# Six Strassen pairs per MLP instead of four, squares on ScalarE, and eight low parts made by ScalarE and an adding DMA

## The chip, the cores and the metric

The kernel runs on one core of one Trainium2 chip. The metric is the device time of one execution, in microseconds; three runs of the kernel before took 555.92, 555.95 and 556.19 us. Beside them one execution was taken by the hardware profiler.

## The reference

A causal decoder trunk of two layers on 256 tokens of width 1024, in float32. Layer 0 mixes tokens with block-sparse attention of 16 heads (one block of 256 here), layer 1 with dilated attention of 12 heads in three groups. Each mixer is followed by a squared-ReLU MLP, and each of the four sub-layers is post-normalised:

```python
def sq_relu_mlp(x, w_in, w_out):                 # w_in 1024 x 4096, w_out 4096 x 1024
    return jnp.square(jax.nn.relu(x @ w_in)) @ w_out

for i in range(2):
    mix = moba_attention(h, ...) if i % 2 == 0 else dilated_attention(h, ...)
    h = layer_norm(2 ** 0.5 * h + mix, ...)
    h = layer_norm(2 ** 0.5 * h + sq_relu_mlp(h, w_in[i], w_out[i]), ...)
```

(2 ** 0.5 is DEEPNORM_ALPHA for a depth of 2.)

## The kernel before

**Split numbers.** Every large product is made of three products of a faster float type: an operand a is stored as a high part (rounded) and a low part (a minus its high part), and a*b is taken as hi*hi + hi*lo + lo*hi. `split` (line 378) does this: ScalarE (ACT) copies the source into the high tile (line 380), VectorE (DVE) subtracts (line 385). `load_w` (394) brings one weight tile of 128 x 1024 (512 KB) into a "raw" buffer with a DMA of the SP queue and splits it into a "whi" and a "wlo" tile. There are 7 raw buffers and 10 of each of the others.

**The MLP** (class `Mlp`, 1062) works on the 4096 hidden columns in eight chunks of 512. `head` does the x @ w_in part of chunk 0 in a token-major form while the LayerNorm ahead of the MLP is being finished. A step "f" followed by a chunk's number does it for one other chunk (`do_first`): four weight tiles of 128 hidden columns each, products into four "tp" banks of PSUM (`mm_wstat_wide`, 523: 8 of 512 columns and 8 of 256 for each tile), and behind each bank `relu_sq` (1040): an ACT copy of half the bank, a DVE addition, and a DVE operation that takes max(u, 0) * u. `relu_sq_T` splits the result into "ahi" and "alo".

A step "o" (`do_out`) is the second matmul of one chunk: four weight tiles of w_out, each with 24 / 2 = 12 products of 512 columns (two halves of tokens m, two halves of the output columns, three terms; `mm_rows`, 637) into the four "acc" banks. The tiles of the tail (`ntail`, the last 4 of MLP 0 and 6 of MLP 1) wait for `out_and_ln` (998), which does the four banks one after the other so that the LayerNorm of token half 0 (`ln_half`, 961) can start while half 1 is still on TensorE. In the last MLP half 1 has a form of its own: a right part of 256 columns, the left 512, and the last 256 on top of what DVE puts into a further bank; then `ln_last` (930).

**Strassen pairs.** Two weight tiles (256 hidden units) against two halves of tokens and two halves of columns are a 2 x 2 block product. A step "S" (`do_duo`, 1121) does it with seven block products of three terms (21 products of 512 columns) instead of eight (24). Before that, four sums of blocks of weights are made by DVE and split (`load_duo`, 597), and four sums of blocks of activations (`duo_sums`, 572). Four of the seven products collect in the four "tp" banks over all Strassen pairs of the MLP, so no "f" step can come after the first S; step "z" (`combine`, 1139) adds them to the residual rows, one ACT copy and eight DVE operations. Chunks 4 and 5 are done in this way:

```python
STEPS = ("f1 o0 f2 o1 f3 o2 f4 f5 f6 f7 S40 o3 S42 o6 S50 S52 z o7",) * 2   # written twice in the file
```

**What sets the order.** The program text makes a list of operations with their reads and writes. `Plan.order` (179) gives each a due time and plays them through a model of the engines; on each engine the ready one with the earliest due time goes first. TensorE's due times follow the program text, and the loads on SP stay in its order. The stores of the last LayerNorm's half 0 are given due times 8 and 7 us ahead of the end (`store`, 926, `early`). The resulting order is written out for each engine; waits are semaphores. At step f4 the kernel also loads the LayerNorm's g and b, and in MLP 0 the rope table and the mask of layer 1.

Behind MLP 0's last products TensorE goes on with `layer1_head` (1276): the first value projection of layer 1 for token half 0.

Of the kernel before, what the change touches and what calls it, by code (L numbers as in the profile page):

```python
# [319 lines left out]
def tile_trunk(  # L320
# [248 lines left out]
    def split_part(n, src, sk, hi, lo, hk, lk, sbuf=True):  # L569
        split(n, src, hi, lo, sk, hk, lk, sbuf=sbuf)  # L570

    def duo_sums(hk, hk2):

        a11, a21 = part(hk, S, P), part(hk, S + P, P)
        a12, a22 = part(hk2, S, P), part(hk2, S + P, P)
# [1 line left out]
        s1, s2, s3, s4 = [part(s, i * P, P) for i in range(4)]
        rk, rk2 = [(hk, 1)], [(hk2, 1)]
        tt(P, s3, a11, a21, ALU.subtract, rk, [(s, 2)])
        tt(P, s1, a21, a22, ALU.add, rk + rk2, [(s, 0)])  # L580
        tt(P, s2, a22, s3, ALU.subtract, rk2 + [(s, 2)], [(s, 1)])
        tt(P, s4, a12, s2, ALU.subtract, rk2 + [(s, 1)], [(s, 3)])
        tags = [duo_tags[(len(duo_used) * 4 + i) % len(duo_tags)] for i in range(4)]
        duo_used.append(s)
        (ph, pl), (sh, sl) = [[mk([P, 512], F32R, *tags[2 * i + h]) for h in range(2)] for i in range(2)]
        split(P, a11, part(ph, 0, P), part(pl, 0, P), rk, [(ph, 0)], [(pl, 0)], sbuf=True)
        split(S, part(hk2, S, S), part(ph, P, S), part(pl, P, S), rk2, [(ph, 1)], [(pl, 1)], sbuf=True)
        split(512, lambda: s.t, lambda: sh.t, lambda: sl.t, [(s, i) for i in range(4)], [(sh, 0)], [(sl, 0)], sbuf=True)
        one = [(ph, pl, i * P, int(i > 0)) for i in range(3)]
        four = [(sh, sl, i * P, 0) for i in range(4)]  # L590
        return one + four

    duo_tags = [("sc0", 4), ("sc0", 4), ("sc0", 4), ("sc0", 4), ("sc1", 4), ("sc1", 4), ("sc1", 4), ("sc1", 4),
                ("v", 4), ("v", 4), ("v", 4), ("v", 4), ("q0hi", 1), ("q0lo", 1), ("q1hi", 1), ("q1lo", 1)]
    duo_used = []

    def load_duo(x_src, y_src, single):

        x = mk([P, 1024], F32, "raw", NRAW)
        dma(lambda: x.t, x_src, (), [(x, 0)], P * 1024 * 4)  # L600
        b11, b12 = part(x, 0, 512), part(x, 512, 512)
# [1 line left out]
        split(512, b11, part(hi, q * 512, 512), part(lo, q * 512, 512), [(x, 0)], [(hi, q)], [(lo, q)], sbuf=True)
        y = load_w(y_src)
        b22, b21 = part(y.raw, 0, 512), part(y.raw, 512, 512)
        yk = [(y.raw, 0)]
        ts = [mk([P, 512], F32, tag, 2) for tag in ("pt0", "pt1", "pt0", "pt1")]
        t1, t3, t2, t4 = ts
        pairs = [[mk([P, 1024], F32R, tag, NSLOT) for tag in ("whi", "wlo")] for _ in range(2)]

        def put(t, i):
            h, l = pairs[i // 2]
            c = i % 2
            split(512, lambda: t.t, part(h, c * 512, 512), part(l, c * 512, 512), [t], [(h, c)], [(l, c)], sbuf=True)
            return h, l, c * 512, c

        whole = lambda t: (lambda: t.t)
        tt(512, whole(t1), b12, b11, ALU.subtract, [(x, 0)], [t1])
        tt(512, whole(t3), b22, b12, ALU.subtract, yk + [(x, 0)], [t3])
        w5, w7 = put(t1, 0), put(t3, 1)  # L620
        tt(512, whole(t2), b22, whole(t1), ALU.subtract, yk + [t1], [t2])
        w6 = put(t2, 2)
        tt(512, whole(t4), b21, whole(t2), ALU.subtract, yk + [t2], [t4])
        w4 = put(t4, 3)
        return (hi, lo, q * 512, q), (y.hi, y.lo, 512, 0), (y.hi, y.lo, 0, 0), w4, w5, w6, w7
# [406 lines left out]
    def relu_sq_T(ps, ahi, alo, j):  # L1032
        both, hk = relu_sq(ps)
        keys = [(j, 0), (j, 1)]
        split(
            S, part(both, S, S), lambda: ahi.t[:, j, :], lambda: alo.t[:, j, :], hk,
            [(ahi, k) for k in keys], [(alo, k) for k in keys], sbuf=True,
        )

    def relu_sq(ps):  # L1040
        both = mk([P, 512], F32, "ta", NTA)
        u, h = (lambda: both.t[:, :S]), (lambda: both.t[:, S:])
        uk, hk = [(both, 0)], [(both, 1)]
        op("ACT", act(S), lambda: nc.scalar.activation(u(), ps.t[:, S:], AF.Copy), [ps], uk)  # L1044
        tt(S, u, lambda: ps.t[:, :S], u, ALU.add, [ps] + uk, uk)
        stt(S, 0, h, u, lambda: 0.0, u, ALU.max, ALU.mult, uk, hk)
        return both, hk
# [14 lines left out]
    class Mlp:  # L1062
# [17 lines left out]
        def rest(self, between):  # L1080
# [8 lines left out]
            def do_out(c):
                for j in range(4):  # L1090
                    pos = c * 4 + j
                    item = ((*chunks[c], j), load_w(wout[i][pos]), pos, nkt)
                    if nkt - pos <= ntail:
# [383 lines left out]
```

## Time and profile before

| | |
|---|---|
| median of three runs | 555.95 us |
| the profiled execution | 556.29 us |
| its span, first to last instruction | 554.5 us |
| TensorE busy, instructions | 545.1 us, 3211 |
| DVE busy, instructions | 464.1 us, 849 |
| ACT busy, instructions | 317.8 us, 534 |
| POOL (GpSimd) busy, instructions | 9.4 us, 15 |
| granted TensorE clock | 0.997 |
| DMA | 105.62 MB, mean 190 GB/s |

The difference of 1.8 us between execution and span lies before the first and behind the last instruction. "PE" in the rows is TensorE's products, "PEld" its loads of stationary operands, which overlap them. A product's row shows its latency; the distance from one to the next is shorter. A letter and digits such as L385 name the line of the kernel, and `wlo<-raw,whi` the tile written and the tiles read. "<-" behind an idle time names what ended the wait.

### The profile page before, as it was taken

The page shows a single profiled execution, that of the slowest core. Times are in us where ns is not written, and L with a number is a line of the kernel's source. Part 1 is how long each engine was busy: PE and PEld are TensorE (multiplying, and loading weights), DVE is VectorE, ACT ScalarE, POOL GpSimd, SP SyncE. Part 2 cuts the span into 40 slices and gives each one's busy share as a digit, 9 for nine tenths or more (in the row PEclk, how much of TensorE's full clock was granted, in tenths as well). Part 3 has the DMA queues.
Part 4 walks back from the last instruction along what each step waited for, and adds up shares of the span by engine and source line. Part 5 has one row for each costly group of instructions (what it writes and reads, how often), then busy time and mean ns, then how long its engine had stood idle before and what let it go on. Part 6 is the DMA issues. An engine that isn't in the chain of part 4 may idle for free.

```text
span 554.5 us, 8668 instructions
## 1 busy us (share of the span) xinstructions
PE 545.1 (98%) x3211; PEld 465.6 (84%) x3211; DVE 464.1 (84%) x849; ACT 317.8 (57%) x534; POOL 9.4 (2%) x15
## 2 busy tenths in 40 slices
PE   9999999999999999999998999999999999999995
PEld 7988888888888888988887889888888888888884
DVE  5898999897673859999899999889748458999976
ACT  5667897257555464756643567645654555566700
POOL 0000000000000000000000000000000000000001
PEclk9999999999999999999999999999999999999998
DMA  8996147548875715575615745534786372657102
GB/s 316 333 367 232 58 134 239 217 124 292 279 257 169 245 59 194 169 251 202 218 68 154 304 152 189 160 108 135 293 293 224 135 249 72 190 192 213 56 1 76
DMA packets 30282, 105.62 MB, mean 190 GB/s; under 512 B 3360, under 2 KB 4256, under 8 KB 30240
## 3 DMA queue, kind: packets, MB, share of 16 engines
q1 hardware_dynamic: 29664, 104.35, 55.5%
q10 hardware_dynamic: 576, 0.72, 0.4%
q8 instruction: 25, 0.41, 0.3%
q14 instruction: 17, 0.14, 0.1%
HBM read 104.01 MB, written 1.05 MB: 189 GB/s over the span
## 4 chain that ended last, share of the span: by engine, by line
PE 97%; DVE 1%; DMA 1%; POOL 0%; issue 0%; DVEq 0%; ACT 0%; POOLq 0%
PE acc L389 54%; PE tp L389 41%; PE tp L798 3%; DVE tok L664 1%; DMA raw<-in_xw_dram 1%; POOL rstd L912 0%; DVE wlo L385 0%; DVEq L1471 0%; DVE bst L970 0%; DVE mv L910 0%; DVE bst L943 0%; ACT xs L380 0%; DVE rstd L915 0%; POOLq L955 0%; POOLq L912 0%
## 5 line engine op out<-in xcount | busy, mean ns | idle before, releaser
L380 ACT ACTIVATE whi<-raw 128x1024 fp32r<-128x1024 f32 (+2 forms) x184 | 184.1, 1022 | 89.8 <-PE acc L389 49.5
L385 DVE TENSOR_TENSOR wlo<-raw,whi 128x1024 fp32r<-128x1024 f32 (+3 forms) x186 | 213.1, 1168 | 18.6 <-ACT whi L380 17.7
L389 PE MATMUL tp<-xs,whi 128*128 128x512 f32 x448 | 104.8, 390 | 0.0
L389 PEld LDWEIGHTS tp<-xs,whi 128*128 128x128 f32 x448 | 83.6, 188 | 17.0
L389 PE MATMUL acc<-whi,ahi 128*128 128x512 f32 (+1 forms) x248 | 96.7, 390 | 0.0
L389 PE MATMUL acc<-wlo,ahi 128*128 128x512 f32 (+1 forms) x248 | 96.0, 387 | 0.0
L389 PE MATMUL acc<-whi,alo 128*128 128x512 f32 (+1 forms) x248 | 83.0, 387 | 0.0
L389 PE MATMUL acc<-xs,whi 128*128 128x512 f32 (+1 forms) x272 | 57.2, 357 | 0.3 <-ACT xs L380 0.3
L389 PEld LDWEIGHTS tp<-xs,wlo 128*128 128x128 f32 x448 | 55.6, 192 | 1.1
L389 PE MATMUL tp<-xs,wlo 128*128 128x256 f32 x448 | 55.9, 283 | 0.0
L657 DVE TENSOR_TENSOR ta<-tp,ta 128x256 f32<-128x256 f32 (+1 forms) x60 | 26.1, 439 | 35.5 <-ACT ta L1044 34.2
L389 PEld LDWEIGHTS acc<-whi,alo 128*128 128x128 f32 x248 | 46.6, 188 | 9.6
L389 PEld LDWEIGHTS acc<-whi,ahi 128*128 128x128 f32 x248 | 46.6, 188 | 9.3 <-issue 0.3
L389 PEld LDWEIGHTS acc<-wlo,ahi 128*128 128x128 f32 x248 | 46.6, 188 | 9.0
L389 PEld LDWEIGHTS acc<-xs,whi 128*128 128x128 f32 x272 | 44.8, 191 | 7.6 <-ACT xs L380 1.1
L1044 ACT ACTIVATE ta<-tp 128x256 f32<-128x256 f32 x56 | 21.4, 382 | 25.8 <-PE tp L389 25.7
L389 PE MATMUL acc<-xs,wlo 128*128 128x256 f32 x224 | 30.7, 284 | 0.0
L389 PEld LDWEIGHTS acc<-xs,wlo 128*128 128x128 f32 x224 | 29.3, 192 | 0.9
L389 PE MATMUL acc<-whi,xs 128*128 128x512 f32 (+1 forms) x112 | 28.7, 366 | 0.0
L380 ACT ACTIVATE whi<-pt 128x512 fp32r<-128x512 f32 x32 | 19.3, 626 | 11.6 <-DVE pt L657 11.3
L380 ACT ACTIVATE ahi<-ta 128x256 fp32r<-128x256 f32 x40 | 16.0, 412 | 17.3 <-DVE ta L664 17.3
L389 PE MATMUL tp<-whi,xs 128*128 128x512 f32 x80 | 25.2, 396 | 0.0
(162 smaller groups left out, 657.2 us busy)
## 6 DMA issues: line engine op xcount, KB each, us to landing
raw<-in_win_dram SPq DMA_DIRECT2D x64, 512.0 KB, 4.4
raw<-in_wout_dram SPq DMA_DIRECT2D x64, 512.0 KB, 4.4
raw<-in_wqk_dram SPq DMA_DIRECT2D x22, 512.0 KB, 8.0
raw<-in_wo_dram SPq DMA_DIRECT2D x14, 512.0 KB, 4.2
raw<-in_wv_dram SPq DMA_DIRECT2D x8, 512.0 KB, 6.3
g<-in_lng_dram SPq DMA_DIRECT2D x4, 512.0 KB, 6.9
b<-in_lnb_dram SPq DMA_DIRECT2D x4, 512.0 KB, 7.3
raw<-in_wv1a_dram SPq DMA_DIRECT2D x4, 512.0 KB, 3.8
```

The source lines that it names most:

```text
L380: op("ACT", act(n, sbuf=sbuf), lambda: nc.scalar.activation(hi(), src(), AF.Copy), r, whi)
L385: lambda: nc.vector.tensor_tensor(lo(), src(), f32(hi()), op=ALU.subtract), list(r) + list(whi), wlo,
L389: nc.tensor.matmul(out_ap, lhsT, rhs, start=start, stop=stop)
L657: op("DVE", dve(n) + extra, lambda: nc.vector.tensor_tensor(out_ap(), a(), b(), op=alu), r, w)
L664: lambda: nc.vector.scalar_tensor_tensor(dst(), a(), s(), b(), op0=o0, op1=o1), r, w,
L798: nc.tensor.transpose(ps.t[:, c : c + P], src(), ident.t)
L1044: op("ACT", act(S), lambda: nc.scalar.activation(u(), ps.t[:, S:], AF.Copy), [ps], uk)
```

## The change

- **Six pairs by Strassen.** Steps now name pairs of weight tiles, 0 to f in hexadecimal: o and O plain, s and S by Strassen. Both MLPs have Strassen pairs 2, 4, 6, 8, a and d. A capital letter means that the activations are split as soon as they are there (into tiles that belong to the attention stages: v, q, sc, pt, ahi, alo, handed out by `Cells`); a small letter that they are kept in float32 and split just before use, into "ta" buffers.
- **The form of the sums** is another, with the same count: four sums of weights (512 columns) made in place in the two raw buffers, and four of activations (128 columns); the splits are fewer and larger (one of 512 and three of 1024 for the weights).
- **Squares.** The two banks of a pair are put side by side, and ACT takes Relu and then Square over 512 columns in place (SQUARES is all "A"); DVE's max-and-multiply is gone.
- **Far tiles.** For pairs 5 and 14 (four weight tiles per MLP) the low part is no longer a DVE subtraction: ACT writes minus the high part into the low tile, and a DMA issued by POOL adds the weights to it from HBM once more.
- **Tail.** What stands behind z, pairs c and f, is the tail in both MLPs: four tiles. z itself comes after O7 and o9.
- **Loads.** The LayerNorm's g and b (and rope and mask) are still loaded at f4, which is now the second step.

```diff
 STEPS = (
-    "f1 o0 f2 o1 f3 o2 f4 f5 f6 f7 S40 o3 S42 o6 S50 S52 z o7",
-    "f1 o0 f2 o1 f3 o2 f4 f5 f6 f7 S40 o3 S42 o6 S50 S52 z o7",
-)
-DUO = (4, 5)
+    "f5 f4 f2 f3 O0 f7 f1 O5 f6 ob s2 S8 Oe S4 sa S6 O1 O3 sd O7 o9 z oc Of",
+) * 2
+FAR = (5, 14)
+FAR_OUT = lambda ap: ap
+SQUARES = ("A" * 16,) * 2
...
+DMA_SUMS = 0.0
+GB_AT = "f4"
+MASK_AT = "f4"
+CELLS = [("v", 4)] * 4 + [("q0hi", 1), ("q0lo", 1), ("q1hi", 1), ("q1lo", 1)] + [("sc0", 4)] * 4 + [("sc1", 4)] * 4 + [
+    ("pt0", 2), ("pt1", 2)] * 2
+BIG = [("ahi", 3), ("alo", 3)] * 2
...
+    def load_far(src):
+        w = W()
+        w.raw = mk([P, 1024], F32, "raw", NRAW)
+        w.hi = mk([P, 1024], F32R, "whi", NSLOT)
+        w.lo = mk([P, 1024], F32R, "wlo", NSLOT)
+        dma(lambda: w.raw.t, src, (), [(w.raw, 0)], P * 1024 * 4)
+        op("ACT", act(1024, sbuf=True), lambda: nc.scalar.activation(w.hi.t, w.raw.t, AF.Copy), [(w.raw, 0)], [(w.hi, 0)])
+        op("ACT", act(1024, sbuf=True), lambda: nc.scalar.activation(w.lo.t, f32(w.hi.t), AF.Copy, scale=-1.0), [(w.hi, 0)], [(w.lo, 0)])
+        op("POOL", 1.2, lambda: nc.gpsimd.dma_start(FAR_OUT(w.lo.t), src, accum_op=ALU.add), (), [(w.lo, 0)], xfer=P * 1024 * 8)
+        return w
...
+    def spare():
+        return mk([P, 512], F32R, "ta", NTA), 0, 0
+
+    def duo_sums(u, cells):
...
+        tt(P, s3, a11, a21, ALU.subtract, [(t, 0)], [(s, 0)])
+        tt(P, r2, a22, s3, ALU.add, [(t, 1), (s, 0)], [(s, 1)])
+        tt(P, s4, a12, r2, ALU.subtract, [(t, 1), (s, 1)], [(s, 2)])
+        tt(P, a21, a21, a22, ALU.subtract, [(t, 0), (t, 1)], [(t, 0)])
+        uh, ul, sh, sl = cells or [spare() for _ in range(4)]
+        split_to((t, c0, (0, 1)), uh, ul, 512)
+        split_to((s, 0, (0, 1, 2)), sh, sl, 384)
...
+    def load_duo(pair, single):
...
+        split(512, x0, part(hi, q * 512, 512), part(lo, q * 512, 512), xk[:1], [(hi, q)], [(lo, q)], sbuf=True)
...
+        w3, w2 = wide(y, 0)
...
+            tt(512, x0, x0, x1, ALU.add, xk, xk[:1])
+            tt(512, x1, x1, y0, ALU.add, xk[1:] + yk[:1], xk[1:])
+        w5, w7 = wide(x, 1)
+        tt(512, y0, y0, x0, ALU.add, yk[:1] + xk[:1], yk[:1])
+        tt(512, y1, y1, y0, ALU.add, yk, yk[1:])
+        w6, w4 = wide(y, 2)
...
+    def relu_sq(banks, u, eng):
+        t, c0, _ = u
+        for i, ps in enumerate(banks):
+            c = part(t, c0 + i * S, S)
+            op("ACT", act(S), lambda c=c, ps=ps: nc.scalar.activation(c(), ps.t[:, S:], AF.Copy), [ps], [(t, i)])
+            tt(S, c, lambda ps=ps: ps.t[:, :S], c, ALU.add, [ps, (t, i)], [(t, i)])
+        both = [(t, 0), (t, 1)]
+        c = part(t, c0, 512)
+        if eng == "A":
+            op("ACT", act(512, 0, True), lambda: nc.scalar.activation(c(), c(), AF.Relu), both, both)
+            op("ACT", act(512, 0, True), lambda: nc.scalar.activation(c(), c(), AF.Square), both, both)
+        else:
+            stt(512, 0, c, c, lambda: 0.0, c, ALU.max, ALU.mult, both, both)
...
+            def do_out(p, late):
+                for k, get in enumerate(do_pair(p)):
+                    item = (get, (load_far if p in FAR else load_w)(wout[i][p][:, k * 1024 : k * 1024 + 1024]), 2 * p + k, nkt)
+                    if late:
                         tail.append(item)
                     else:
                         for m in range(2):
                             mm_rows(acc[m], item, m)
...
+            late_ = False
+            for step in steps:
+                c = int(step[1], 16) if len(step) > 1 else 0
+                if step == GB_AT:
                     gb = load_gb(2 * i + 1)
...
+                if step[0] == "f":
+                    do_first(c)
+                elif step[0] in "oO":
+                    do_out(c, late_)
+                elif step[0] in "sS":
+                    do_duo(c)
                 else:
                     combine()
+                    late_ = True
             out_and_ln(acc, tail, len(tail), gb, self.last, between, 1.0)
...
-    nc = _bacc.Bacc("TRN2", target_bir_lowering=False, num_devices=1, dynamic_dma_scratch_size=256)
+    nc = _bacc.Bacc("TRN2", target_bir_lowering=False, num_devices=1, dynamic_dma_scratch_size=512)
```

More of the change, by code (lines that the diff above doesn't have):

```diff
@@ L27 @@
 NEG = -1.0e30
-BIG = 3.0e38
+HUGE = 3.0e38
 NCH = DFF // 512
@@ L567, in part @@
         return lambda: t.t[:, c0 : c0 + n]
[L569 to L575, printed above, removed]
-        s = mk([P, 512], F32, "ta", NTA)
[L577 to L601, printed above, removed]
-        hi, lo, q = single
[L603 to L625, printed above, removed]
@@ new lines, in tile_trunk, with __init__, take, give @@
+    class Cells:
+        def __init__(self):
+            self.small = list(CELLS)
+            self.big = list(BIG)
+            self.half = []
+        def take(self, dtype, wide=False):
+            if wide and not self.half and self.big:
+                tag = self.big.pop(0)
+                b = mk([P, 1024], F32R, *tag)
+                self.half = [(b, 0, tag), (b, 512, None)]
+            if wide and self.half:
+                b, c0, tag = self.half.pop(0)
+                return b, c0, c0 // 512
+            if self.small:
+                tag = self.small.pop(0)
+                return mk([P, 512], dtype, *tag), 0, 0
+            raise ValueError("cells")
+        def give(self, cells):
+            for b, c0, _ in cells:
+                if (b.tag, 3) in BIG:
+                    if c0:
+                        self.big.append((b.tag, 3))
+                else:
+                    self.small.append(next(x for x in CELLS if x[0] == b.tag))
@@ L651, in mm_rows @@
             "PE", 3 * sum(p[2] / 2400 + 0.0135 for p in pieces), go,
-            [(w.hi, 0), (w.lo, 0), (ahi, (j, m)), (alo, (j, m)), *behind], [p[0] for p in pieces],
+            [(w.hi, 0), (w.lo, 0), *ak, *behind], [p[0] for p in pieces],
         )
@@ L1030, in out_and_ln @@
             ln_half([p[0] for p in acc[m]], m, gb, last, AHEAD["turn"][m], alpha)
[L1032 to L1047, printed above, removed]
+    def relu_sq(banks, u, eng):
+        t, c0, _ = u
+        for i, ps in enumerate(banks):
[7 more added lines that the diff above has]
+            op("ACT", act(512, 0, True), lambda: nc.scalar.activation(c(), c(), AF.Square), both, both)
+        else:
+            stt(512, 0, c, c, lambda: 0.0, c, ALU.max, ALU.mult, both, both)
     def relu_sq_tok(ps, m, ahi, alo):
@@ L1085, in rest @@
             ntail = TAIL[2 * i + 1]
-            pend = list(range(nx))
             tail = []
[L1089 to L1093, printed above, removed]
+            cells = Cells()
+            kinds = kinds_of(i)
+            held = {}
+            steps = STEPS[i].split()
+            prods = []
+            left = [sum(x[0] in "sS" for x in steps)]
@@ new lines, in do_first @@
+            def do_first(c):
+                for js in GROUPS:
+                    tiles = [(psum("tp"), load_w(win[i][c * 4 + j])) for j in js]
+                    mm_wstat_wide(tiles)
+                    for k in range(0, len(js), 2):
+                        p = 2 * c + js[k] // 2
+                        n = {"O": 2, "S": 4}.get(kinds[p], 0)
+                        u = cells.take(F32) if not n else (mk([P, 512], F32, "ta", NTA), 0, 0)
+                        homes = [cells.take(F32R, True) for _ in range(n)]
+                        taken[p] = homes or [u]
+                        relu_sq([ps for ps, _ in tiles[k : k + 2]], u, SQUARES[i][p])
+                        held[p] = u, homes
+                        if n:
+                            ready(p)
@@ new lines, in rest, with do_pair @@
+            taken = {}
+            def do_pair(p):
+                if p < 2 * nx:
+                    gets = [rows_of(*chunks[p // 2], p % 2 * 2 + k) for k in range(2)]
+                else:
+                    if kinds[p] in "os":
+                        ready(p)
+                    gets = held[p]
+                    cells.give(taken[p])
+                return gets
+            def do_out(p, late):
+                for k, get in enumerate(do_pair(p)):
+                    item = (get, (load_far if p in FAR else load_w)(wout[i][p][:, k * 1024 : k * 1024 + 1024]), 2 * p + k, nkt)
+                    if late:
@@ L1136, in do_duo @@
                     mm_duo(bank, a, w, bool(own and first), bool(own and final))
-                done[0] += 1
             def combine():
```

144 lines of the change are left out of this document (87 added, 57 removed).

## The prediction

> **What bounds the kernel now.** I read the page first, then who waited for whom on TensorE, then the chain that ended last.
>
> ```profile
> span 554.5 us, 8668 instructions
> PE 545.1 (98%) x3211; PEld 465.6 (84%) x3211; DVE 464.1 (84%) x849; ACT 317.8 (57%) x534; POOL 9.4 (2%) x15
> ```
>
> A busy PE need not stream at its best pace, so two more views matter. The first gives TensorE's waits (total, times, longest):
>
> ```profile
> PE tp L798 <- DVE tok L664: 1.2, 1, 1.2
> PE tp L389 <- PEq L1462: 0.8, 1, 0.8
> PE acc L389 <- ACT xs L380: 0.3, 1, 0.3
> PE acc L389 <- DVE wlo L385: 0.2, 1, 0.2
> ```
>
> The chain in order of time (start, us, what):
>
> ```profile
> 136.83 10.91 PE acc L389 x48
> ...
> 407.12 11.09 PE tp L389 x64
> ```
>
> In the whole execution TensorE waits 2.5 us. The chain gives its pace: 48 products of 512 columns in 10.91 us are 0.2273 us each; a chunk of the first MLP matmul (32 of 512 and 32 of 256 columns) takes 11.09 us. So TensorE's work is the time, and a product that is left out is worth its 0.227 us as long as the others still feed it. The profiled execution took 556.29 us, 1.8 us more than its span; it lies 0.34 us above the median 555.95. I work out a difference and take it from the median.
>
> **Term 1, products removed.** A plain pair of weight tiles costs 24 products (5.46 us), a Strassen pair 21 (4.77 us). Two more Strassen pairs in each of two MLPs: 4 x 3 x 0.2273 = **-2.73 us**.
>
> **Term 2, the end of the last MLP.** Before, its last six weight tiles were kept for the tail, in which row half 0 finishes first and its LayerNorm runs on DVE under the products of half 1. Now only the steps behind z, "oc" and "Of", are kept: four tiles. So the cover gets shorter. The timeline of TensorE at the end, and of DVE:
>
> ```profile
> 538.69 0.39 PE L389 MATMUL acc<-whi,alo 128*128 128x512 f32 x1
> 541.20 0.40 PE L389 MATMUL acc<-whi,ahi 128*128 128x512 f32 x1
> 545.31 0.28 PE L389 MATMUL tp<-whi,ahi 128*128 128x256 f32 x1
> 547.34 0.28 PE L389 MATMUL tp<-whi,alo 128*128 128x256 f32 x1
> ```
>
> ```profile
> 539.12 0.69 DVE L664 SCALAR_TENSOR_TENSOR tok<-tok,acc 128x512 f32<-128x512 f32 x1 [0.62 <-PE acc L389]
> 543.53 0.42 DVE L664 SCALAR_TENSOR_TENSOR tp<-tok,acc 128x256 f32<-128x256 f32 x1
> 543.86 0.42 DVE L664 SCALAR_TENSOR_TENSOR tok<-tok,acc 128x256 f32<-128x256 f32 x1
> 545.51 0.69 DVE L664 SCALAR_TENSOR_TENSOR tok<-tok,acc 128x512 f32<-128x512 f32 x1 [0.58 <-PE acc L389]
> 546.23 0.75 DVE L940 BATCH_NORM_STATS2 bst<-tok 128x6 f32<-128x256 f32 x2
> 547.66 0.43 DVE L943 BATCH_NORM_STATS2 bst<-tp 128x6 f32<-128x256 f32 x1 [0.67 <-PE tp L389]
> 548.12 0.26 DVE L910 BATCH_NORM_AGGREGATE mv<-bst 128x2 f32<-128x24 f32 x1
> ```
>
> Call x the end of half 0's products: 538.69 + 0.23 = 538.92. DVE is done with half 0 at 543.53, x + 4.61, and only then turns to half 1, which finds it free 0.58 us before it is needed. Half 1 has 18 products each in three groups: 2.28, 4.11 and, with 0.12 for the last, 2.15 us. With four tiles they are 12 each: 1.52, 2.74 and 1.43. The second group now ends at x + 4.26, but the third adds to a bank that DVE writes at 543.53, so it starts at x + 4.61 + 0.42 + 0.05 = x + 5.08: TensorE waits 0.8 us and ends at x + 6.5. DVE goes on with the right part (from 543.86, x + 4.94; 1.65 us to the next row less 0.58 idle) until x + 6.01, then the left part and its statistics (545.51 to 546.98, 1.47), then the last statistics (0.46 to the next start): the aggregation starts at x + 7.94 instead of 548.12, x + 9.20. Behind it nothing differs. x itself stays: 2.73 us earlier by term 1, and two tiles' share of half 1 (12 products, 2.73) comes ahead of it. The end thus moves by -1.26 us. Two tiles' share of half 1 takes 2.73 us in the wide form and took 8.54 / 3 = 2.85 in three groups, which saves 0.12; so the shorter cover costs 2.73 + 0.12 - 1.26 = **+1.59 us**.
>
> **Term 3, the turn between the layers.** All but 1.1 us of TensorE's waiting lies behind the first MLP; TensorE's timeline there, and DVE's:
>
> ```profile
> 292.67 1.32 PE L798 MATMUL tp<-ident,tok 128*128 128x128 f32 x8 [1.18 <-DVE tok L664]
> ...
> 294.47 0.50 PE L389 MATMUL acc<-wlo,xs 128*128 128x512 f32 x1 [0.25 <-DVE wlo L385]
> ```
>
> ```profile
> 276.40 0.69 DVE L657 TENSOR_TENSOR ta<-tp,ta 128x512 f32<-128x512 f32 x1
> ...
> 281.75 0.67 DVE L657 TENSOR_TENSOR tok<-tp,tok 128x512 f32<-128x512 f32 x1
> ...
> 293.20 1.22 DVE L385 TENSOR_TENSOR wlo<-raw,whi 128x1024 fp32r<-128x1024 f32 x1
> ```
>
> TensorE's filler there, the next layer's first value projection, stops half way because the low part of a weight tile comes only at 293.20; DVE was busy before with combining the Strassen products (up to 282.42) and both LayerNorm halves. In the new order O7 and o9 (10.9 us) stand between the last Strassen pair and z, so the combination can be done before half 0 is finished. That gives DVE back eight operations of 0.69, 5.5 us: the low part can come early, the filler goes on, and the 1.43 us of waiting can go. Bounds: -1.43, and 0 if DVE fills the place with other splits. I take **-1.0**, nearer the first, since one split of 1.22 us is all that is missing.
>
> **Costs beside TensorE, taken as 0.** First three stretches (busy us of PE, PE's weight loads, DVE, ACT and POOL, granted clock, DMA share, GB/s): an MLP, its Strassen part, its start; then rows of DVE's timeline and SP's.
>
> ```profile
> 126.60:288.80 162.20, 162.20 (x828) 138.86 (x827) 129.64 (x214) 93.78 (x142) 0.99 (x1) 1.00 0.61 202
> 236.15:288.80 52.65, 52.65 (x237) 43.66 (x237) 49.32 (x76) 30.12 (x42) 0.99 (x1) 1.00 0.58 191
> 121.60:136.80 15.20, 15.20 (x85) 13.20 (x85) 11.20 (x14) 11.17 (x15) 0.00 (x0) 1.00 0.85 277
> ```
>
> ```profile
> 382.25 4.62 DVE L385 TENSOR_TENSOR wlo<-raw,whi 128x1024 fp32r<-128x1024 f32 x4
> ...
> 260.80 1.89 DVE L385 TENSOR_TENSOR wlo<-pt,whi 128x512 fp32r<-128x512 f32 x3
> ...
> 118.67 5.80 SPq L376 DMA_DIRECT2D raw<-in_win_dram  x4
> ```
>
> The groups by line and shape (busy, mean ns | idle before); the two last are of the stretch 191.7 to 236.15, f4 to f7; and two DMA issues (KB, us to landing):
>
> ```profile
> L664 DVE SCALAR_TENSOR_TENSOR ta<-ta 128x256 f32<-128x256 f32 x56 | 22.8, 419 | 0.1
> L657 DVE TENSOR_TENSOR ta<-ta,ta 128x128 f32<-128x128 f32 x24 | 6.7, 286 | 0.1
> L380 ACT ACTIVATE whi<-raw 128x1024 fp32r<-128x1024 f32 x170 | 176.0, 1057 | 86.7 <-PE acc L389 47.6 <-PE tp L389 23.0 <-issue 8.0
> L1044 ACT ACTIVATE ta<-tp 128x256 f32<-128x256 f32 x56 | 21.4, 382 | 25.8 <-PE tp L389 25.7
> L1052 ACT ACTIVATE ta<-ta 128x512 f32<-128x512 f32 x4 | 2.5, 632 | 0.1
> ```
>
> ```profile
> L385 DVE TENSOR_TENSOR wlo<-pt,whi 128x512 fp32r<-128x512 f32 x4 | 2.7, 689 | 0.0
> L385 DVE TENSOR_TENSOR wlo<-raw,whi 128x512 fp32r<-128x512 f32 x1 | 0.7, 686 | 0.0
> ```
>
> ```profile
> raw<-in_wout_dram SPq DMA_DIRECT2D x64, 512.0 KB, 4.4
> ...
> m<-in_mask_dram SPq DMA_DIRECT2D x1, 512.0 KB, 9.3
> ```
>
> Four splits of 1024 in 4.62 us, the last 1.22 long, follow each other by 1.13; of 512 by 0.60. DVE, per MLP: squaring leaves it (28 x 0.41 = -11.4), four low parts too (-4.5); two pairs become Strassen pairs, each with four sums of 0.60, 1.5 x 1.13 more of weight splits and four sums of 0.29: +10.5. So some 5 less of 129.6 in 162 us: no bound on average. ACT gains 14 x 2 x 0.632 and 4 x 1.06, with splits some 22 us on 93.8: no bound either. The new homes of the activations, tiles of the attention, are all read before the tail is over, so the next layer finds them free. In one f chunk ACT has 4 x 1.06 + 4 x 0.38 + 4 x 0.63 and up to 1.8 of splits, 10.1 of 11.09 us; it lies beside TensorE. If that cover is gone, each 0.1 us more is 0.1 us in up to 14 chunks.
>
> The Trainium skill (ScalarE: Activation LUTs, Rules for kernel authors) sends relu and multiplications to VectorE, up to three times as fast in bf16. Here the fp32 row has ACT at 0.632 us against DVE's 0.68 to 0.69 for 512 columns; at three times DVE's time a chunk would need 15.8 us of ACT, and 14 chunks would cost 14 x 4.7 = +66 us. The trace speaks against the rule for this type.
>
> The g and b loads, and in the first MLP rope and mask, now stand ahead of f4's weights on SP. The old f1's loads start at 118.67, and TensorE is done with f1 at 136.83, where f4 is due now. f5 (2.1 MB), these 1.8 MB and f4's first tile (0.5) take 15.9 us at the 277 GB/s of that stretch, its split 1.06: ready at 135.6, cost 0. At the 202 GB/s of the whole MLP, which no transfer there was bound by, it would be 141.5, +4.7. I take the rate of the same place, 0; a gain is excluded, as no load is waited for now.
>
> The adding DMA has no row. It loads 512 KB and reads its target: from below one plain load, 4.4 us from issue to landing; from above two of the slowest such load, 18.6; nearest is twice 4.4, 8.8. O5's tiles get their places when f7's weights go, one f1 (11.1 us) ahead; less two ACT passes (2.1) 9.0 us are left: cost 0, at the lower end 0, at the upper end 9.6 us at O5 and some 7 at Oe, +33 in all. POOL has nothing queued behind but the LayerNorm powers, over 60 us later.
>
> For that DMA the Trainium skill (DMA: Bandwidth & Descriptors, Anatomy of one DMA) fits 2.0 us + bytes/436e3, an estimate of 4.4 us for 1 MB moved; by it the term stays 0. No run here shows it yet.
>
> **Sum**: -2.73 - 0.12 + 1.59 - 1.0 = -2.26; 555.95 - 2.26 = **553.7 us**.
>
> **The rivals.** *A, DVE becomes the bound from s2 to S6* (slower). A Strassen pair needs 0.60 + 3 x 1.13 + 4 x 0.60 = 6.4 us of DVE, a late one (small letter) 2.2 more for four sums of 0.29 and two splits, against 4.77 of TensorE. ob, s2, S8, Oe, S4, sa, S6 need 2.9 + 8.6 + 6.4 + 0 + 6.4 + 8.6 + 6.4 = 39.3; S6's last weights are due 30.0 + 3.4 us after f6. At the 94% that DVE reached in the old stretch (49.32 of 52.65) it does 31.4, so 7.9 us must be prepared before f6 ends. Ten places of weights hold f6's four, ob's two and s2's four: 8.7 us of work, enough by a little. For it: the margin of 0.8, and ob and a late pair want seven of six "ta" buffers. Against it: the old kernel had its first Strassen pair split before f7 ended (the x4 and x1 rows, from 191.7 to 236.15). If half of s2's weights (3.2) are not ready, 2.4 us are missing in each MLP: 553.7 + 4.8 = 558.5. It turns slower than before from 1.1 us per MLP on.
>
> *B, the adding DMA lands late*: at 10 us instead of 9.0, 1.0 at each O5: 555.7, no difference. *C, the gain is eaten*: no gain at the turn, and some 0.5 us of new waits: 555.2, within what a measurement tells apart. *D, DVE takes half 1 first at the end*, which term 2 excludes by the order seen in the rows: then 552.1, with the turn's full gain 551.7. That the change does not do what it says is not to be feared: the steps hold six letters s or S, and pairs 5 and 14 have two tiles each.
>
> **How the numbers follow.** Forecast 45% (553.2 with the whole turn, 554.7 with none of it), D 8%, C 15%, B 10%, A 22%. A change under 0.2% (1.1 us) can't be told from none with this kernel. Faster: the forecast but for its slowest part, and D: 51%. Same: the rest of it, C and B but for a late tail: 25%. Slower: A and that tail: 24%. Range 551.7 (D) to 558.5 (A).
>
> **What would show it.** Right: TensorE's streaming time down by 2.85 us; the aggregation of the last LayerNorm some 8.0 us behind half 0's last product, with a wait of about 0.8 us of TensorE for DVE before the last group; the waits at the turn under 0.5 us; none in the MLPs. Wrong: waits of TensorE for wlo in s2 to S6 (A), for the DMA at O5 or Oe (B), or for raw loads at f4. A time over 555 means that A, B or C holds.

## The result, and the profile after

The changed kernel is slower: 560.32 us (559.34 to 561.68) against 555.98, a ratio of 1.0079, 95% interval 1.0058 to 1.0101. The forecast was 553.7, with a range up to 558.5. The profiled execution took 559.34 us, the shortest of the four, with a span of 557.5. From the page of the changed kernel:

```profile
span 557.5 us, 8613 instructions
PE 544.3 (98%) x3193; PEld 464.0 (83%) x3193; DVE 458.3 (82%) x785; ACT 353.0 (63%) x566; POOL 16.6 (3%) x23
```

TensorE has 18 instructions fewer (it had 3211), DVE 64. Who waited for whom on TensorE (total, times, longest):

```profile
PE acc L403 <- DMA wlo<-in_wout_dram: 5.2, 2, 3.0
PE tp L403 <- PEq L1554: 0.8, 1, 0.8
```

The waits for DVE and ACT that the old kernel had behind MLP 0 are gone. In their place stand two for the adding DMA that makes the low part of a far tile. TensorE's timeline at both places (start, duration, idle before):

```profile
228.91 0.39 PE L403 MATMUL acc<-whi,sc 128*128 128x512 f32 x1
229.42 0.50 PE L403 MATMUL acc<-wlo,sc 128*128 128x512 f32 x1
...
234.77 0.39 PE L403 MATMUL acc<-whi,sc 128*128 128x512 f32 x1
237.38 0.50 PE L403 MATMUL acc<-wlo,sc 128*128 128x512 f32 x1 [2.22 <-DMA wlo<-in_wout_dram]
...
492.84 0.39 PE L403 MATMUL acc<-whi,sc 128*128 128x512 f32 x1
496.21 0.80 PE L403 MATMUL acc<-wlo,sc 128*128 128x512 f32 x1 [2.98 <-DMA wlo<-in_wout_dram]
...
499.72 0.40 PE L403 MATMUL acc<-wlo,sc 128*128 128x512 f32 x1
```

Both are at step Oe (pair 14), at the second of its two tiles. The first one's low part is only just late, and in MLP 0 alone: 228.91 to 229.42 are 0.51 us instead of 0.227. POOL's timeline shows why the second is later:

```profile
175.51 1.03 POOL L417 DMA_DIRECT2D wlo<-in_wout_dram  x1 [59.91 <-PE acc L403]
184.15 0.90 POOL L417 DMA_DIRECT2D wlo<-in_wout_dram  x1 [7.60 <-ACT ta L1102]
219.05 0.88 POOL L417 DMA_DIRECT2D wlo<-in_wout_dram  x1 [34.00 <-ACT wlo L416]
229.69 0.90 POOL L417 DMA_DIRECT2D wlo<-in_wout_dram  x1 [9.76 <-issue]
...
478.45 0.87 POOL L417 DMA_DIRECT2D wlo<-in_wout_dram  x1 [33.99 <-PE acc L403]
487.81 0.88 POOL L417 DMA_DIRECT2D wlo<-in_wout_dram  x1 [8.49 <-PE tp L403]
```

The second adding DMA of each pair is issued 8.6 to 10.6 us after the first. Its operands were long ready: ACT's minus pass for the one of 229.69 (a row of ACT's timeline) ended at 221.16, and the profile names no releaser for it but "issue".

```profile
220.12 1.04 ACT L416 ACTIVATE wlo<-whi 128x1024 fp32r<-128x1024 f32 x1
```

The trace has a time of landing for each of these DMAs. The four first ones landed at 183.89, 229.37, 443.26 and 487.50, and the second of each pair is issued 0.26 to 0.32 us later. So the second is issued when the first has landed. The chain of waits has the two second ones of Oe (start, duration):

```profile
229.69 7.64 DMA wlo<-in_wout_dram
...
487.81 8.35 DMA wlo<-in_wout_dram
```

The list of DMA issues has all eight (KB each, median us to landing; the shortest took 5.9, the longest 10.3):

```profile
wlo<-in_wout_dram POOLq DMA_DIRECT2D x8, 512.0 KB, 8.4
```

In MLP 1 the wait costs more than its 2.98 us. The product that waited and the eight behind it start from 496.21 to 499.72, 3.51 us, where eight steps of 0.2273 would take 1.82. A window from the end of the wait (busy us of PE, weight loads, DVE, ACT and POOL; then the granted clock, the DMA share and GB/s) shows why:

```profile
496.22:499.63 3.41, 3.41 (x8) 2.73 (x9) 3.41 (x7) 1.25 (x2) 0.00 (x0) 0.50 0.76 220
```

For 3.41 us the granted clock is half, which is 1.7 us of products; from 499.63 on it is 1.00 again.

**Where the time went.** Four points cut an execution into three stretches: the four small transposes of "ta" that stand early in each MLP's first f step, the eight transposes of "tok" that open the turn behind MLP 0, and the last aggregation. TensorE's rows of before and after:

```profile
126.91 0.60 PE L798 MATMUL tp<-ident,ta 128*128 128x128 f32 x4
287.02 1.03 PE L798 MATMUL tp<-ident,tok 128*128 128x128 f32 x8
386.54 0.60 PE L798 MATMUL tp<-ident,ta 128*128 128x128 f32 x4
```

```profile
126.59 0.60 PE L864 MATMUL tp<-ident,ta 128*128 128x128 f32 x4
288.28 1.03 PE L864 MATMUL tp<-ident,tok 128*128 128x128 f32 x8
386.02 0.60 PE L864 MATMUL tp<-ident,ta 128*128 128x128 f32 x4
```

With the aggregation at 548.12 before and 551.01 after, and the same points of every other kernel:

| kernel | median, us | MLP 0 | turn and layer 1's attention | MLP 1 |
|---|---|---|---|---|
| before | 555.98 | 160.11 | 99.52 | 161.58 |
| after | 560.32 | 161.69 | 97.74 | 164.99 |
| after without far tiles | 551.94 | 158.78 | 97.72 | 160.14 |
| far tiles only at O5 | 551.95 | 158.78 | 97.73 | 160.17 |
| far: O5 and one tile of Oe | 552.91 | 158.97 | 97.73 | 160.54 |
| no far, four Strassen pairs | 553.94 | 160.14 | 97.73 | 161.52 |
| after, six raw buffers | 560.78 | 162.93 | 98.88 | 163.53 |
| the same, more descriptor room | 553.16 | 159.20 | 98.89 | 160.16 |
| no far, z straight behind sd | 558.80 | 158.79 | 101.70 | 163.23 |
| no far, six tiles in the tail | 551.59 | 256.51 for both | | 160.24 |
| no far, squares on DVE | 551.86 | 158.75 | 97.74 | 160.15 |
| no far, seven pairs | 552.65 | 158.77 | 99.78 | 159.47 |
| seven pairs, far, room, six raw | 554.88 | 159.12 | 100.98 | 159.49 |
| no far, six pairs and seven | 550.64 | 158.77 | 97.73 | 159.47 |

(With six tiles in the tail the transposes of the turn stand elsewhere, so its first two stretches are given as one; the kernel without far tiles has 256.50 there.)

The far tiles cost 161.69 - 158.78 = 2.91 us in MLP 0 and 164.99 - 160.14 = 4.85 in MLP 1. The rows account for it. MLP 0: 237.38 - 234.77 less one step of 0.23 is 2.38, 229.42 - 228.91 less one step 0.28, and the restart after each wait about 0.1. MLP 1: 496.21 - 492.84 less one step 3.14, and 499.72 - 496.21 less eight steps 1.69; together 4.83.

### The profile page after: what moved, and what is told of

Read it like the earlier page. It is cut to its first block, busy times and chain, and to the rows that moved or that the text cites. A ratio compares the mean times of both kernels' runs of the same rounds, so it can differ in the third digit from the quotient of the medians.

```text
span 557.5 us, 8613 instructions
## 1 busy us (share of the span) xinstructions
PE 544.3 (98%) x3193; PEld 464.0 (83%) x3193; DVE 458.3 (82%) x785; ACT 353.0 (63%) x566; POOL 16.6 (3%) x23
## 4 chain that ended last, share of the span: by engine, by line
PE 94%; DMA 3%; issue 1%; DVE 1%; ACT 0%; POOL 0%; DVEq 0%; POOLq 0%
PE acc L403 51%; PE tp L403 40%; DMA wlo<-in_wout_dram 3%; PE tp L864 3%; DMA raw<-in_xw_dram 0%; DVE tok L730 0%; POOL rstd L978 0%; ACT whi L394 0%; DVEq L1563 0%; DVE bst L1006 0%; ACT xs L394 0%; DVE bst L1009 0%; DVE mv L976 0%; DVE bst L989 0%; POOLq L1021 0%
## 5 line engine op out<-in xcount | busy, mean ns | idle before, releaser
L399 DVE TENSOR_TENSOR wlo<-raw,whi 128x1024 fp32r<-128x1024 f32 (+2 forms) x202 | 229.2, 1162 | 16.6 <-ACT whi L394 13.8
L403 PE MATMUL acc<-whi,ta 128*128 128x512 f32 (+1 forms) x132 | 44.5, 387 | 0.0
L403 PE MATMUL acc<-whi,ahi 128*128 128x512 f32 x104 | 41.1, 395 | 0.0
L403 PE MATMUL acc<-wlo,ahi 128*128 128x512 f32 x96 | 37.4, 390 | 0.0
L403 PE MATMUL acc<-whi,alo 128*128 128x512 f32 x96 | 34.2, 390 | 0.0
L403 PE MATMUL acc<-whi,sc 128*128 128x512 f32 (+1 forms) x98 | 34.0, 397 | 0.0
L403 PEld LDWEIGHTS acc<-whi,ta 128*128 128x128 f32 x132 | 24.7, 188 | 4.9
L723 DVE TENSOR_TENSOR ta<-tp,ta 128x256 f32<-128x256 f32 (+1 forms) x36 | 15.9, 450 | 14.5 <-ACT ta L1102 14.4
L403 PE MATMUL acc<-wlo,ta 128*128 128x512 f32 (+1 forms) x66 | 25.5, 386 | 0.0
L403 PE MATMUL acc<-wlo,sc 128*128 128x512 f32 (+1 forms) x48 | 19.6, 408 | 5.3 <-DMA wlo<-in_wout_dram 5.2
L850 ACT ACTIVATE sc<-sc,mx 128x256 f32<-128x256 f32 (+2 forms) x40 | 19.8, 498 | 6.1 <-DVE mx L840 5.7
```

The source lines that it names most:

```text
L399: lambda: nc.vector.tensor_tensor(lo(), src(), f32(hi()), op=ALU.subtract), list(r) + list(whi), wlo,
L403: nc.tensor.matmul(out_ap, lhsT, rhs, start=start, stop=stop)
L723: op("DVE", dve(n) + extra, lambda: nc.vector.tensor_tensor(out_ap(), a(), b(), op=alu), r, w)
L850: lambda: nc.scalar.activation(e(), e(), AF.Exp, bias=bias(), scale=-1.0, accum_out=total()), r, w,
```

## The experiments

The theory after the result: six pairs and the new turn gain more than forecast, and the far tiles at Oe cost all of it and 4 us more, because two adding DMAs don't run side by side. Each experiment changes the changed kernel ("after"), or the kernel without far tiles where it says so; the run before the last one changes the kernel with seven pairs.

**No far tiles.** DVE makes all low parts again.

```diff
-FAR = (5, 14)
+FAR = ()
```

> No adding DMA at all: all low parts are DVE subtractions again (FAR is empty), the rest as in the changed kernel. Theory (the adding DMAs of pair 14 land late and cost TensorE 2.2 us in the first MLP and 3.0 us plus 1.7 us of slow clock in the second): the profiled 559.3 less 6.9, so 552 to 553 us, and no wait of TensorE in the MLPs. Rival (the far tiles hold up the Strassen stretch because DVE is short of time there): TensorE waits for wlo tiles instead, 2 to 5 us in each MLP, and the time stays above 556 us.

551.94 us (551.08 to 552.18), ratio to before 0.9922 [0.9907, 0.9936]. TensorE's only wait in its list beside the 0.8 us at the start of the execution, and ten us of the Strassen part (busy us of PE, weight loads, DVE, ACT, POOL):

```profile
PE acc L403 <- ACT xs L394: 0.2, 1, 0.2
```

```profile
225.00:235.00 10.00, 10.00 (x46) 8.29 (x45) 9.93 (x15) 4.96 (x6) 0.00 (x0) 1.00 0.36 115
```

The far tiles are the whole loss. DVE is busy 9.93 of these 10 us, and TensorE never waits for it: the work done ahead is enough, even with four low parts more per MLP than in the changed kernel. The far tiles relieved an engine that nobody waited for.

**Far tiles only at O5.**

```diff
-FAR = (5, 14)
+FAR = (5,)
```

> Adding DMAs for pair 5 alone. Theory (only pair 14's come late): the same 552 to 553 us as without any. Rival (each adding DMA costs something wherever it stands, by slowing the other loads or by landing late): half of the loss stays, 555 to 557 us, with a wait at O5.

551.95 us (551.68 to 552.12), ratio 0.9926 [0.9909, 0.9942], no wait in the MLPs. POOL's timeline:

```profile
175.59 1.03 POOL L417 DMA_DIRECT2D wlo<-in_wout_dram  x1 [59.92 <-PE acc L403]
185.03 0.90 POOL L417 DMA_DIRECT2D wlo<-in_wout_dram  x1 [8.41 <-ACT ta L1102]
```

Here too the second is issued 9.4 us behind the first, but O5's products come late enough to hide both: 158.78 and 160.17 us, as without far tiles.

**Four Strassen pairs, all else as without far tiles.**

```diff
-    "f5 f4 f2 f3 O0 f7 f1 O5 f6 ob s2 S8 Oe S4 sa S6 O1 O3 sd O7 o9 z oc Of",
+    "f5 f4 f2 f3 O0 f7 f1 O5 f6 ob s2 S8 Oe S4 oa S6 O1 O3 od O7 o9 z oc Of",
-FAR = (5, 14)
+FAR = ()
```

> As without adding DMAs, and the pairs a and d done plainly, so four Strassen pairs per MLP as before. Theory (a Strassen pair is worth its three products, TensorE stays the bound): 2.7 us above the run without adding DMAs, so about 555.3 us. Rival (the sums and splits of two more pairs cost as much as they save): not above that run.

553.94 us (553.83 to 554.74), ratio 0.9964 [0.9951, 0.9977]. The two pairs are worth 160.14 - 158.78 = 1.36 us in MLP 0 and 161.52 - 160.14 = 1.38 in MLP 1, six products of 0.2273 each (2.74 together; 2.7 was expected). The medians differ by 2.00 only: in the two profiled executions MLP 0 starts at 127.40 and at 126.30 us, and the edit changes nothing ahead of it. Against before, both MLPs are as long as they were (160.14 to 160.11, 161.52 to 161.58), and only the turn is shorter, by 1.79.

**One far tile at Oe.** Pair 5 keeps both, pair 14 only its first.

```diff
-(load_far if p in FAR else load_w)
+(load_far if p in FAR and (p == 5 or k == 0) else load_w)
```

> Pair 5 as in the changed kernel, of pair 14 only the first tile by an adding DMA, the second by DVE. Theory (in the trace the second adding DMA is issued only when the first has landed, 8 to 10 us later, and it is that one that is late): the waits at Oe fall from 5.2 us to under 0.6 and the time to 552 to 554 us. Rival (a single adding DMA is late already at that place): 555 us or more with a wait of over 1 us at Oe in each MLP.

552.91 us (552.17 to 554.48), ratio 0.9946 [0.9928, 0.9963]. The chain of waits of this kernel at Oe of MLP 1:

```profile
476.37 10.05 DMA wlo<-in_wout_dram
```

Alone, the DMA is on the edge: issued at 476.37, landed at 486.42, 0.2 us after TensorE could have used it. The waits of 2 and 3 us are gone, so they belong to the second DMA. The runs scatter by 2.3 us, against 0.4 with far tiles at O5 only.

**More room for descriptors, and its control.** The program sets `dynamic_dma_scratch_size` to 512, which is taken here as the bytes per partition for the descriptors of POOL's DMAs; the runs don't show what is kept there. One kernel has 4096, and one raw buffer goes to make the place. The control has the six raw buffers alone. The two have the same instructions in the same order on every engine.

```diff
-NRAW = 7
+NRAW = 6
...
-dynamic_dma_scratch_size=512
+dynamic_dma_scratch_size=4096
```

> The changed kernel with 4096 instead of 512 bytes of descriptor room for POOL's DMAs, and one raw buffer fewer (6) to make the place; all four far tiles per MLP stay. Theory (the second adding DMA of a pair is issued only when the first has landed, because the room for its descriptors holds one): now the second one is issued right behind ACT's minus pass, 1.5 to 4 us after the first instead of 8.6 to 10.6, and TensorE's waits of 2.2 and 3.0 us at Oe go. Time 552 to 554 if six raw buffers cost nothing. Rival (POOL or its queue takes one adding DMA at a time whatever the room): gaps of 8 to 10 us and waits of 2 to 3 us as before, 559 to 562.

```diff
-NRAW = 7
+NRAW = 6
```

> The control for the kernel with more descriptor room: the changed kernel with 6 raw buffers and the room of 512 bytes as it was. Both theories: the second adding DMA of a pair 8 to 10 us behind the first, TensorE waits 2 to 3 us at Oe in each MLP, 559 to 562. If six raw buffers alone shift the issues so that the waits go, the time is 552 to 554 and the other kernel proves nothing.

With the room 553.16 us (552.93 to 553.45), ratio 0.9950 [0.9933, 0.9966]; without it 560.78 (558.95 to 561.33), 1.0080 [1.0061, 1.0099]. POOL's timeline with the room:

```profile
218.94 0.88 POOL L417 DMA_DIRECT2D wlo<-in_wout_dram  x1 [40.28 <-ACT wlo L416]
221.41 0.88 POOL L417 DMA_DIRECT2D wlo<-in_wout_dram  x1 [1.60 <-ACT wlo L416]
...
476.95 1.82 POOL L417 DMA_DIRECT2D wlo<-in_wout_dram  x2 [40.48 <-PE acc L403]
```

POOL's timeline in the control, and then what TensorE waited for there:

```profile
219.22 0.89 POOL L417 DMA_DIRECT2D wlo<-in_wout_dram  x1 [35.06 <-ACT wlo L416]
229.45 0.90 POOL L417 DMA_DIRECT2D wlo<-in_wout_dram  x1 [9.35 <-issue]
```

```profile
PE acc L403 <- DMA wlo<-in_wout_dram: 5.2, 2, 3.1
```

With the room the second DMA is issued 2.5 us behind the first in MLP 0, released by ACT's minus pass, and directly behind it in MLP 1, and no wait for it is listed. So the size of this room is the cause, and neither POOL nor its queue takes one adding DMA at a time. Run side by side they take longer (median 9.9 us to landing, 7.6 in the control) and still come in time, but for the first one at Oe of MLP 0, which is 0.3 us late, as in the changed kernel. Six raw buffers cost 1.2 us in the stretch with layer 1's attention in both kernels (98.9 against 97.7); less that, the kernel with the room is no better than the one without far tiles.

**The combination next to the last Strassen pair** (without far tiles).

```diff
-    "... S6 O1 O3 sd O7 o9 z oc Of"
+    "... S6 O1 O3 O7 o9 sd z oc Of"
```

> No far tiles, and the last Strassen pair behind O7 and o9, next to z: '... S6 O1 O3 O7 o9 sd z oc Of'. Theory of term 3 (the turn gains because the combination is out of DVE's way before half 0 is finished): from the first transposed half of MLP 0 to the end of the turn again 32.3 us instead of 30.5 (+1.4 to +1.8, as waits of TensorE on tok and on a low part), and at the end of MLP 1 another 0.5 to 2 us, since eight operations of 0.69 us fall into the 5.5 us of half 0's tail: 554 to 556 against 551.9. Rival (the turn gains by what ACT took over from DVE): 551.9 plus or minus 0.4, turn 30.5.

558.80 us (557.80 to 558.95), ratio 1.0047 [1.0032, 1.0062], more than expected. TensorE's waits, two rows of DVE's timeline at the turn, and two windows, at the turn and at the end of MLP 1:

```profile
PE acc L403 <- DVE wlo L399: 2.3, 1, 2.3
PE tp L403 <- DVE tp L730: 2.1, 1, 2.1
```

```profile
281.04 0.67 DVE L723 TENSOR_TENSOR tok<-tp,tok 128x512 f32<-128x512 f32 x1
...
290.64 1.22 DVE L399 TENSOR_TENSOR wlo<-raw,whi 128x1024 fp32r<-128x1024 f32 x1
```

```profile
293.73:297.73 4.00, 4.00 (x16) 3.38 (x15) 4.00 (x6) 2.14 (x3) 0.00 (x0) 0.72 0.55 205
...
548.00:550.00 2.00, 2.00 (x12) 1.80 (x11) 2.00 (x6) 0.00 (x0) 0.00 (x0) 0.64 0.00 0
```

The combination reaches into half 0's LayerNorm (281.04), the low part that the filler of the turn needs is made at 290.64, and TensorE waits 2.33 us for it (in the old kernel 0.25, behind 1.18 for tok). At the end it waits 2.15 us for the bank that DVE writes ahead of the last group. Both waits are followed by a lower clock, and the stretches lose 3.98 and 3.09 us. The edit moves the sums and splits of the last pair towards the turn together with the combination, so it doesn't tell which of the two DVE lacked the time for.

**Six tiles in the tail** (without far tiles).

```diff
-    "... sd O7 o9 z oc Of"
+    "... sd O7 z o9 oc Of"
```

> No far tiles, and o9 behind z, so that both tails have six tiles instead of four: '... sd O7 z o9 oc Of'. Term 2 as predicted (four tiles are too short a cover for half 0's LayerNorm and cost 1.59 us): 1 to 1.6 us less than with four, 550.4 to 551. Theory now (with four tiles TensorE put six products of o9's second tile for half 1 behind half 0, and DVE, free of the squares and of the combination, kept up; the last aggregation stands 0.66 us behind TensorE's end in both): 551.9 plus or minus 0.3.

551.59 us (551.31 to 552.13), ratio 0.9922 [0.9907, 0.9937]; the stretches are the same as with four tiles (256.51 to 256.50, 160.24 to 160.14). The shorter tail costs nothing.

**Squares on DVE** (without far tiles).

```diff
-SQUARES = ("A" * 16,) * 2
+SQUARES = ("D" * 16,) * 2
```

> No far tiles, and the squares back on DVE (one max-and-multiply of 512 columns, 0.69 us, for each pair instead of ACT's Relu and Square): 14 x 0.69 = 9.7 us more on DVE and 17.7 less on ACT per MLP. In the kernel without far tiles DVE is busy 67 of the 87 us of the f steps, but 9.9 of every 10 us from f6 to S6, with no wait on TensorE. Theory: only what falls behind the last f steps counts, at most two squares (1.4 us) per MLP, and a lead hides it: 551.9 to 552.6, no waits for a low part of DVE. Rival (DVE is at the edge, as rival A of the prediction had it): every square near f6 shows, waits for low parts of 1.4 us or more in each MLP, 554.5 and above.

551.86 us (551.37 to 552.07), ratio 0.9925 [0.9910, 0.9940]. Which engine makes the squares makes no difference here, in either direction.

**Seven pairs** (without far tiles).

```diff
-    "... S6 O1 O3 sd O7 o9 z oc Of"
+    "... S6 O1 s9 O3 sd O7 z oc Of"
```

> No far tiles, and pair 9 by Strassen too (seven per MLP, '... S6 O1 s9 O3 sd O7 z oc Of'). TensorE: another 3 x 0.2273 = 0.68 us less per MLP, so 550.6 if DVE feeds it. DVE: a late pair needs 8.6 us where o9 needed 2.3, so 6.3 more in a stretch where it was busy 99%, with 6.3 us idle only behind the combination. Theory (DVE is the next bound): waits of TensorE for low parts before O3, sd or O7, 1 to 6 us per MLP, and a later combination: 553 to 560. Rival (DVE's lead takes it): no waits, 550.6.

552.65 us (552.46 to 553.22), ratio 0.9942 [0.9927, 0.9957]. Neither theory: TensorE's list has

```profile
PE acc L403 <- DVE wlo L399: 1.9, 2, 1.6
```

and both waits stand at the turn, the longer one here:

```profile
290.33 0.50 PE L403 MATMUL acc<-wlo,xs 128*128 128x512 f32 x1 [1.62 <-DVE wlo L399]
```

MLP 1 is 159.47 us long, 0.67 shorter than with six pairs, which is the three products. DVE feeds seven pairs; what it has no time left for is the low part of the filler, once one step less stands between the last Strassen pair and z. Between the combination and half 0 it makes one low part here, against six with six pairs. From the start of MLP 0 to that of MLP 1 the kernel needs 258.55 us instead of 256.50, although it leaves out the same three products there.

**Seven pairs with far tiles, room and six raw buffers** (against the seven pairs alone).

```diff
-FAR = ()
+FAR = (5, 14)
-NRAW = 7
+NRAW = 6
-dynamic_dma_scratch_size=512
+dynamic_dma_scratch_size=4096
```

> Seven pairs, with the far tiles of pairs 5 and 14, the larger descriptor room and six raw buffers. The far tiles take 4 x 1.13 = 4.5 us per MLP off DVE, half of it in the full stretch. Theory (far tiles pay only where DVE is the bound): the waits for DVE's low parts are 2 us or more per MLP shorter than with seven pairs alone, so the time is lower than there in spite of the 1.2 us that six raw buffers cost: 551.5 to 556. Rival (the far tiles never pay): the same or slower than seven pairs alone.

554.88 us (554.02 to 555.54), ratio 0.9976 [0.9965, 0.9987]. The waits for DVE's low parts are the same 1.9 us as with seven pairs alone, and six raw buffers cost what they cost before. The far tiles don't pay here either. That the work which they take from DVE lies too far ahead of the place where DVE is late is argued, not shown.

**Six pairs in MLP 0, seven in MLP 1, no far tiles.**

```diff
 STEPS = (
     "f5 f4 f2 f3 O0 f7 f1 O5 f6 ob s2 S8 Oe S4 sa S6 O1 O3 sd O7 o9 z oc Of",
-) * 2
+    "f5 f4 f2 f3 O0 f7 f1 O5 f6 ob s2 S8 Oe S4 sa S6 O1 s9 O3 sd O7 z oc Of",
+)
```

> No far tiles, six Strassen pairs in MLP 0 and seven (pair 9 too) in MLP 1. With seven in both, MLP 1 was 0.67 us shorter than with six and only the turn behind MLP 0 lost, 2.06 us. Theory (seven cost only where the combination meets the turn): the kernel without far tiles less 0.67, 551.2 to 551.4, no wait of TensorE in MLP 1 above 0.3 us. Rival (the late combination costs the end of MLP 1 as well in the timed runs): 551.9 or more.

550.64 us (550.47 to 551.03), ratio 0.9900 [0.9883, 0.9916]: 97.73 for the turn and 159.47 for MLP 1. It is the fastest of all kernels here, 1.0% faster than before and 1.7% than the changed kernel.

## Why the prediction was wrong

**Term 1 was right.** It said 0.2273 us for each product left out, 1.36 per MLP; 1.36 and 1.38 were measured (four pairs against six).

**Term 2 was mis-sized.** Forecast was +1.59 for the shorter cover, less 0.12. Measured is -0.06 (MLP 1 with four pairs against before), and no gain from six tiles. The rows of the changed kernel's end, TensorE and then DVE:

```profile
543.03 0.39 PE L403 MATMUL acc<-whi,sc 128*128 128x512 f32 x1
543.25 0.39 PE L403 MATMUL acc<-whi,ta 128*128 128x512 f32 x1
...
548.92 0.28 PE L403 MATMUL tp<-whi,ta 128*128 128x256 f32 x1
```

```profile
547.87 0.42 DVE L730 SCALAR_TENSOR_TENSOR tp<-tok,acc 128x256 f32<-128x256 f32 x1
...
551.01 0.26 DVE L976 BATCH_NORM_AGGREGATE mv<-bst 128x2 f32<-128x24 f32 x1
```

Half 0's last product ends its share at x = 543.03 + 0.23 = 543.26, and the aggregation starts at x + 7.75; the forecast had x + 7.94. So the work behind x was nearly right. The step of this term that failed is "two tiles' share of half 1 (12 products, 2.73) comes ahead of it": six of these, those of o9's second tile, stand behind x (from 543.25, 1.36 us). x moves by 1.36 only, and 1.36 + 7.75 - 9.20 = -0.09. The same six products fill the predicted wait of 0.8 us: the bank is written from 547.87, and the group starts at 548.92 without one. Rival D, half 1 first on DVE, did not come about: DVE took half 1 from 547.87 only, 4.61 us behind x, as forecast.

**Term 3 had the mechanism and too small a size.** -1.0 was taken, within -1.43 to 0; -1.78 was measured (97.74 against 99.52), and putting the last pair and its combination back next to the turn brings waits back. DVE's rows of the changed kernel show the place that was gained, the end of the combination, six low parts, and then half 0:

```profile
273.00 0.69 DVE L723 TENSOR_TENSOR tok<-tp,tok 128x512 f32<-128x512 f32 x1
273.61 6.99 DVE L399 TENSOR_TENSOR wlo<-raw,whi 128x1024 fp32r<-128x1024 f32 x6
281.68 0.69 DVE L730 SCALAR_TENSOR_TENSOR tok<-tok,acc 128x512 f32<-128x512 f32 x1 [1.08 <-PE acc L403]
```

The bound was the sum of the waits listed, so it left out what follows them. Of the other 0.35 us, 0.29 can be seen: the eight transposes behind the first wait took 1.32 us, and those of the changed kernel, at 294.42, take 1.03.

**The costs taken as 0.** The squares on ACT were rightly taken as free, and so were the early g and b loads: TensorE's list has no wait at f4. Rival A, DVE as the bound from s2 to S6, fell: with DVE 99% busy, six pairs and even seven in MLP 1 are fed without a wait.

**The adding DMA, a cost taken as 0, was the step that made the time wrong.** Its length was taken as 8.8 us, and 8.4 was measured in the median. The Trainium skill (DMA: Bandwidth & Descriptors, Anatomy of one DMA) gave an estimate of 4.4 for it; the measurement decides for the longer one. But each far pair has two of these DMAs, and the forecast worked out one: it has no step for a second that must wait for the first. At O5 this cost nothing, by luck, since the lead was misread too. The forecast had 9.0 us there; the first DMA was issued at 175.51 and its tile is first used here:

```profile
197.60 0.40 PE L403 MATMUL acc<-wlo,v 128*128 128x512 f32 x1
```

That is a lead of 22.1 us. Both DMAs had landed after 15.2 (at 190.66); the 9.0, with the 2.7 us between the first uses of the two tiles, would not have covered that. At Oe the forecast worked out no lead at all, only a price at the upper end. There the first is issued at 219.05 and the second tile's low part is due one step behind 234.77, 15.9 us later; two DMAs in a row took until 237.38, 18.3 us. Rival B named the right transfer but priced it at the wrong place, O5, and at a quarter of its price (2.0 us where 2.91 + 4.85 were lost); only its sign, a wait at O5 or Oe, named the place. Without the far tiles the kernel takes 551.94, so the other terms together were too cautious by 1.8 us, and the far tiles cost 8.4 us in the medians. Of that, 1.7 us are the half clock behind the wait in MLP 1, for which the forecast had no term.

## What to carry to other kernels

Before work is moved off an engine, look whether anybody waits for it: DVE was 99% busy in the Strassen part and TensorE never waited for it there, so what was moved could gain nothing and brought a deadline of its own. A transfer that is issued in pairs needs its lead checked for the second one, under the assumption that they run one after the other, unless a trace shows them side by side. And where a step of a busy engine moves towards the end of its stage, price what it delays behind it: the seventh pair in MLP 0 left out 0.7 us of products, and on balance MLP 1 started 2.05 us later.
